# An attention kernel: a replanned order of scores, chains of five on VectorE, and first loads in halves

## The chip, the cores and the metric

The kernel runs on one core of one Trainium2 chip. The metric is the device time of one execution in microseconds; a version's time is the median of its runs. The profile's span, from the first to the last instruction, is about 1.75 us shorter than the time of the same execution (kernel before: 397.35 us of time, 395.6 of span). Each run also lists the mean clock granted to TensorE; it turns out to matter. Every run used here is in the fast state, except one single look, whose state is unknown and of which only the head is read, up to the landing of two transposes, the wait for them and the scores that follow.

## The reference

Grouped-query attention: batch 8, 8 query heads, 2 key/value heads, 1024 positions, head dimension 64, float32 in and out.

```
for g in range(n_kv_heads):
    scores = scale * np.matmul(q_group, k_group.transpose(0, 1, 3, 2))
    scores_max = np.max(scores, axis=-1, keepdims=True)
    attn = np.exp(scores - scores_max)
    attn = attn / (np.sum(attn, axis=-1, keepdims=True) + 1e-08)
    output[:, q_start:q_end, :, :] = np.matmul(attn, v_group)
```

## The kernel before

A *job* is one half of a query head (512 queries); a *cell* is one 128x512 block of its scores, 8 cells to a job, 16 to a head, 1024 in all. A cell's exponential is made by ScalarE (two cells per instruction) or by VectorE (one bit-trick instruction per cell, then a chain of four instructions over a group of cells). The score product goes into one of two double-bank buffers for ScalarE (`aps`) or one of two single banks for VectorE (`dps`). The product of the exponentials with V accumulates in `ops` and is normalised by VectorE.

Which engine takes which cell, and the order of every instruction, come from a small simulation in Python, `make_plan`, which always takes what could start first by its own table of durations. The engines then run this fixed order:

```
GROUP = 4
...
    QK, PV, EXP, P1, NORM = 0.214, 0.143, 0.925, 0.605, 0.57
    CHAIN = (0.73, 0.73, 1.26, 1.26)
    FROM_PE, FROM_ACT, FROM_DVE = 0.28, 0.18, 0.12
    LIVE_A, LIVE_D, PENDING, ONLY_A = 26, 6, 8, 14
...
            t, to_d = (ta, 0) if ta <= td else (td, 1)
            if t < INF:
                best = min(best or (INF,), (t, 1 + to_d, "qk", to_d))
```

The first head is loaded in float32 and transposed on TensorE; every later one is cast to bf16 in DRAM by a GpSimd DMA and transposed by two DMAs on the SP queue into `qT`. The head of the program, cut to what is argued about:

```
        for eng, src in ((nc.sync, k[0, 0]), (nc.scalar, q[0, 0])):
            ...                                     # one DMA each
        nc.sync.dma_start(out=vf, in_=v[0, 0]...)
        cast(("q", 0, 1), q[0, 1])                  # GpSimd queue: second head
        for two in range(2):
            nc.gpsimd.tensor_copy(out=vsets[0]..., in_=vf...)   # waits for V
        for side in range(2):
            nc.gpsimd.memset(ksets[1]..., 0.0)
        ...                                         # casts, transposes, copies of K and Q
```

The casts of the third head (0,2), of the next K and so on follow on GpSimd's queue, as planned events.

The softmax here doesn't subtract the row's maximum and nothing guards it: scores larger than these inputs give would overflow.

Of the kernel before, what the change touches and what calls it, by code (L numbers as in the profile page):

```python
# [11 lines left out]

CURVE_A, CURVE_B = 0.32988085, -0.33401025

GROUP = 4


def make_plan(nj, nkc):
# [3 lines left out]



    QK, PV, EXP, P1, NORM = 0.214, 0.143, 0.925, 0.605, 0.57
    CHAIN = (0.73, 0.73, 1.26, 1.26)
    FROM_PE, FROM_ACT, FROM_DVE = 0.28, 0.18, 0.12
    LIVE_A, LIVE_D, PENDING, ONLY_A = 26, 6, 8, 14
    INF = 1e9
    n = nj * nkc  # L30
    ops = []
    pe = act = dve = 0.0
    a_free, bank, obank_free = [0.0, 0.0], [0.0, 0.0], [0.0, 0.0]
# [12 lines left out]
    while normed < nj:  # L46
        best = None
        if nxt < n:
            ta = td = INF
            if open_a is not None:  # L50
                ta = max(pe, open_a["t"])
            elif live["A"] < LIVE_A:
                ta = max(pe, min(a_free))
            if pending < PENDING and nxt < n - ONLY_A and (cur or live["D"] < LIVE_D):
                td = max(pe, min(bank))
            t, to_d = (ta, 0) if ta <= td else (td, 1)
            if t < INF:
                best = min(best or (INF,), (t, 1 + to_d, "qk", to_d))
        for i, s in enumerate(open_jobs):
            for c in rem[s]:  # L60
                at = max(pe, ready.get(s * nkc + c, INF))
                if at < INF:
                    best = min(best or (INF,), (at, 3 + i, "pv", (s, c)))
        if len(open_jobs) < 2 and next_job < nj:
            at = max(pe, min(obank_free), min(ready.get(next_job * nkc + c, INF) for c in range(nkc)))
            if at < INF:
                best = min(best or (INF,), (at, 3 + len(open_jobs), "open", next_job))
        for q, p, kind in ((normq, 0, "norm"), (p1q, 1, "p1"), (chainq, 2, "chain")):
# [1 line left out]
                best = min(best or (INF,), (max(dve, q[0][0]), p, kind, 0))  # L70
        if cur and nxt >= n - ONLY_A and not p1q:
            best = min(best or (INF,), (dve, 9, "flush", 0))
        t, _, kind, arg = best
        if kind == "qk":
            cell = nxt
            nxt += 1
            pe = t + QK
            if not arg:
                if open_a is None:
                    slot = first_free(a_free)  # L80
                    a_id += 1
                    live["A"] += 1
                    open_a = {"slot": slot, "t": a_free[slot], "cells": []}
                    a_free[slot] = INF
                o = open_a
                ops.append((t, "qk", cell, "A", a_id, o["slot"], len(o["cells"])))
                o["cells"].append(cell)
                home[cell] = ("A", a_id)
                if len(o["cells"]) == 2 or nxt >= n:
                    act = max(act, pe + FROM_PE)  # L90
                    ops.append((act, "exp", a_id, tuple(o["cells"])))
                    act += EXP * len(o["cells"]) / 2
                    a_free[o["slot"]] = act + FROM_ACT
                    uses[("A", a_id)] = len(o["cells"])
                    for x in o["cells"]:
                        ready[x] = act + FROM_ACT
                    open_a = None
            else:
                k = first_free(bank)
                bank[k] = INF  # L100
                pending += 1
                ops.append((t, "qk", cell, "D", k, 0, 0))
                p1q.append((pe + FROM_PE, cell, k))
        elif kind == "open":
            o = first_free(obank_free)
            obank[arg] = o
            obank_free[o] = INF
            open_jobs.append(arg)
            rem[arg] = list(range(nkc))
            next_job += 1  # L110
        elif kind == "pv":
            s, c = arg
            cell = s * nkc + c
            opens = len(rem[s]) == nkc
            rem[s].remove(c)
            done = not rem[s]
            ops.append((t, "pv", s, cell, opens, done, obank[s]))
            pe = t + PV
            h = home[cell]
            uses[h] -= 1  # L120
            if not uses[h]:
                live[h[0]] -= 1
            if done:
                open_jobs.remove(s)
                normq.append((pe + FROM_PE, s))
        elif kind == "norm":
            s = normq.pop(0)[1]
            ops.append((t, "norm", s))
            dve = t + NORM
            obank_free[obank[s]] = dve + FROM_DVE  # L130
            normed += 1
        elif kind == "p1":
            _, cell, k = p1q.pop(0)
            if not cur:
                d_id += 1
                live["D"] += 1
            ops.append((t, "p1", cell, k, d_id, len(cur)))
            dve = t + P1
            bank[k] = dve + FROM_DVE
            cur.append(cell)  # L140
            home[cell] = ("D", d_id)
            if len(cur) == GROUP:
                chainq.append((dve, d_id, cur, 0))
                cur = []
        elif kind == "flush":
            chainq.append((dve, d_id, cur, 0))
            cur = []
        else:
            _, g, cells, step = chainq.pop(0)
            ops.append((t, "chain", g, len(cells), step))  # L150
            dve = t + CHAIN[step] * len(cells) / GROUP
            if step + 1 < len(CHAIN):
                chainq.insert(0, (dve, g, cells, step + 1))
            else:
                pending -= len(cells)
                uses[("D", g)] = len(cells)
                for x in cells:
                    ready[x] = dve + FROM_DVE
# [4 lines left out]
def kernel(  # L163
# [25 lines left out]
    NQS = QBS // 128  # L189
    E1 = D + 1  # L190
    PIECE = 256
    scale = 1.0 / math.sqrt(D)
    bits_scale = 128.0 * scale * math.log2(math.e)
    bits_bias = 128.0 * 127.0
# [12 lines left out]
    first_pool = ctx.enter_context(tc.tile_pool(name="firstp", bufs=1))  # L207
    qT_pool = ctx.enter_context(tc.tile_pool(name="qTpool", bufs=8))
    kT_pool = ctx.enter_context(tc.tile_pool(name="kTpool", bufs=4))
    pa_pool = ctx.enter_context(tc.tile_pool(name="papool", bufs=26))  # L210
    pd_pool = ctx.enter_context(tc.tile_pool(name="pdpool", bufs=6))
    tmp_pool = ctx.enter_context(tc.tile_pool(name="tmppool", bufs=2))
    ostage_pool = ctx.enter_context(tc.tile_pool(name="ostage", bufs=10))
    recip_pool = ctx.enter_context(tc.tile_pool(name="recip", bufs=10))
# [24 lines left out]
    qT = {}  # L239
# [48 lines left out]

    def first_loads():

        staged = []
        for eng, src in ((nc.sync, k[0, 0]), (nc.scalar, q[0, 0])):
            f = first_pool.tile([128, NHC, 2, D], FP32, name=f"f{len(staged)}")
            eng.dma_start(
                out=f, in_=src.rearrange("(c p two) d -> p c two d", p=128, two=2)
            )
            staged.append(f)
        vf = first_pool.tile([128, NHC, 2, D], FP32, name="vf")
        nc.sync.dma_start(
            out=vf, in_=v[0, 0].rearrange("(c p two) d -> p c two d", p=128, two=2)  # L300
        )
        cast(("q", 0, 1), q[0, 1])
        for two in range(2):
            nc.gpsimd.tensor_copy(
                out=vsets[0][:, 0, two * NHC : (two + 1) * NHC, 0:D],
                in_=vf[:, :, two, :],
            )
        for side in range(2):
            nc.gpsimd.memset(ksets[1][(1 - side) * D : (2 - side) * D, :, side, :], 0.0)  # L309
        fk, fq = staged  # L310

        hk = first_pool.tile([128, NHC, 3, D], BF16, name="hk")
        nc.vector.tensor_copy(out=hk[:, :, 0:2, :], in_=fk)  # L313
        nc.vector.tensor_copy(out=hk[:, :, 2, :], in_=fk[:, :, 0, :])
        hq = first_pool.tile([128, NHC, 2 * D], BF16, name="hq")
        nc.scalar.copy(out=hq, in_=fq.rearrange("p c two d -> p c (two d)"))
        tk = dbanks[0].tile([128, 2, HALF], BF16, name="dps0")
        tq = dbanks[1].tile([128, HALF], BF16, name="dps1")
        for w in range(2):
            for c in range(NHC):  # L320
                nc.tensor.transpose(  # L321
                    tk[:, w, c * 128 : (c + 1) * 128],
                    hk[:, c, w : w + 2, :].rearrange("p w d -> p (w d)"),
                    ident,
                )
        for c in range(NHC):
            nc.tensor.transpose(tq[:, c * 128 : (c + 1) * 128], hq[:, c, :], ident)
        qT[(0, 0)] = qT_pool.tile([128, HALF], BF16, name="qT")
        lo, hi = slice(0, D), slice(D, 2 * D)
        nc.vector.tensor_copy(out=ksets[0][lo, 0, 0, 0:HALF], in_=tk[lo, 0, :])  # L330
        nc.scalar.copy(out=qT[(0, 0)], in_=tq)
        nc.vector.tensor_copy(out=ksets[0][lo, 0, 0, HALF:S], in_=tk[lo, 1, :])
        nc.vector.tensor_copy(out=ksets[0][hi, 0, 1, 0:HALF], in_=tk[hi, 1, :])
        nc.vector.tensor_copy(out=ksets[0][hi, 0, 1, HALF:S], in_=tk[hi, 0, :])

    p_of = {}
    psum = {}
# [168 lines left out]
```

## Time and profile before

| | before |
|---|---|
| time, median of 4 runs | 397.99 us (397.90 to 398.06) |
| span of the profiled run | 395.6 us |
| ScalarE busy, idle before its exponentials | 381.5 us, 2.1 us |
| VectorE busy, TensorE busy | 375.8 us, 365.7 us |
| first exponential starts, last one ends | 8.16 us, 388.22 us |

In a line of a group, the columns are: source line, engine, operation, output and input tiles with their shapes, count, then busy time in us and mean duration in ns, then idle time of the engine just before these instructions and what ended most of it. The prediction shows these lines.

### The profile page before, as it was taken

Reading aid. Unit: us, or ns where it says so; the run is one execution under the profiler, and the core shown is the slowest. Engines: PE = TensorE matmul, PEld = TensorE weight load, DVE = VectorE, ACT = ScalarE, POOL = GpSimd, SP = SyncE. Lnnn points to the kernel's source line nnn. Section 1 sums busy time; section 2 is a strip of 40 time slices with the busy share of each in tenths; the row PEclk is TensorE's granted clock in tenths of the full one; section 3 lists DMA queues with packets and bytes.
Section 4 is the critical chain, followed back from the end, with each engine's and each line's share of the span. In section 5 each row is a group of like instructions: output and inputs, shape, how many; then the busy total and the mean of one; then the engine's idle time right before and its main releaser. Section 6 shows DMA issues by size and latency. Waiting matters only on the chain.

```text
span 395.6 us, 12683 instructions
## 1 busy us (share of the span) xinstructions
PE 365.7 (92%) x5043; PEld 233.0 (59%) x5132; DVE 375.8 (95%) x664; ACT 381.5 (96%) x415; POOL 86.6 (22%) x165
## 2 busy tenths in 40 slices
PE   4899999999999999999999999999999999999986
PEld 2455566565656556655656565565655666565655
DVE  4999999999999999999999999999999999999995
ACT  4999999999999999999999999999999999999992
POOL 5340303132041313113131040312214131120000
PEclk9999999999999999999999999999999999999999
DMA  4665866749676786847758686785965867574314
GB/s 106 106 125 111 163 107 127 128 86 160 103 139 130 132 143 101 142 90 145 115 103 141 111 141 112 118 143 98 155 109 115 149 132 121 99 130 99 68 28 94
DMA packets 134890, 46.72 MB, mean 118 GB/s; under 512 B 130848, under 2 KB 132384, under 8 KB 133344
## 3 DMA queue, kind: packets, MB, share of 16 engines
q1 hardware_dynamic: 129408, 29.52, 38.3%
q0 software_dynamic: 4896, 16.13, 27.0%
q8 instruction: 40, 0.66, 0.8%
q10 hardware_dynamic: 528, 0.26, 0.2%
q14 instruction: 18, 0.15, 0.2%
HBM read 27.13 MB, written 28.97 MB: 142 GB/s over the span
## 4 chain that ended last, share of the span: by engine, by line
ACT 67%; DVE 11%; PE 10%; issue 6%; DMA 3%; POOL 1%; SPq 0%
ACT pa L362 67%; PE ops L414 5%; PE aps L351 5%; DVE pd L371 3%; DVE y L402 2%; DVE pd L406 2%; DVE ost L429 1%; DMA vf<-in_v_dram 1%; PE dps L351 1%; DVE y L392 1%; DMA qT<-scr_q 1%; POOL kset L309 1%; DVE z L386 1%; DVE rec L427 1%; DMA scr_q<-in_q_dram 1%
## 5 line engine op out<-in xcount | busy, mean ns | idle before, releaser
L362 ACT ACTIVATE pa<-aps 128x1024 bf16<-128x1024 f32 x412 | 379.0, 1064 | 2.1 <-PE aps L351 1.3
L351 PE MATMUL aps<-qT,kset 128*128 128x512 bf16 x735 | 226.2, 379 | 15.5 <-ACT pa L362 13.6
L414 PEld LDWEIGHTS <-pa 128*128 128x128 bf16 x3296 | 134.5, 97 | 57.6 <-DVE ost L429 0.8
L414 PE MATMUL ops<-vset,pa 128*128 128x65 bf16 x3296 | 143.9, 193 | 3.4
L371 DVE TENSOR_SCALAR pd<-dps 128x512 uint16<-128x512 f32 x200 | 129.8, 682 | 2.2 <-PE dps L351 2.2
L351 PEld LDWEIGHTS <-kset 128*128 128x128 bf16 x1024 | 85.3, 97 | 66.3 <-issue 30.9
L248 POOL DMA_DIRECT2D scr_q<-in_q_dram x63 | 34.0, 540 | 173.4 <-PE aps L351 150.6
L351 PE MATMUL dps<-qT,kset 128*128 128x512 bf16 x200 | 64.5, 380 | 1.0
L406 DVE TENSOR_TENSOR pd<-pd,y 128x2048 uint16<-128x2048 uint16 x50 | 61.2, 1225 | 1.7
L402 DVE TENSOR_TENSOR y<-z,y 128x2048 f16<-128x2048 uint16 x50 | 61.2, 1225 | 1.7
L429 DVE TENSOR_TENSOR ost<-ops,rec 128x256 f32<-128x256 f32 x128 | 54.3, 425 | 4.4
L414 PEld LDWEIGHTS <-pd 128*128 128x128 bf16 x800 | 38.5, 97 | 29.8 <-DVE pd L406 7.9
L268 POOL DMA_DIRECT2D kset<-kT x60 | 32.2, 545 | 76.7 <-DMA kT<-scr_k 68.7
L414 PE MATMUL ops<-vset,pd 128*128 128x65 bf16 x800 | 45.3, 194 | 1.2
L392 DVE TENSOR_SCALAR y<-z 128x2048 f16<-128x2048 uint16 x50 | 34.3, 687 | 0.6
L386 DVE TENSOR_SCALAR z<-pd 128x2048 uint16<-128x2048 uint16 x50 | 34.2, 684 | 0.0
L427 DVE RECIPROCAL rec<-ops 128x4 f32<-128x4 f32 x128 | 22.6, 176 | 2.4 <-PE ops L414 1.9
L248 POOL DMA_DIRECT2D scr_v<-in_v_dram x15 | 7.6, 505 | 8.2 <-PE aps L351 7.1
L248 POOL DMA_DIRECT2D scr_k<-in_k_dram x15 | 8.1, 542 | 4.7 <-PE aps L351 4.3
L321 PE MATMUL dps<-ident,hk 128*128 128x128 bf16 x8 | 1.0, 311 | 5.0 <-DVE hk L313 5.0
L321 PEld LDWEIGHTS <-hk 128*128 128x128 bf16 x8 | 0.8, 141 | 5.0 <-DVE hk L313 5.0
L309 POOL MEMSET kset<- 64x2048 bf16 x2 | 3.6, 1798 | 0.1
(20 smaller groups left out, 9.7 us busy)
## 6 DMA issues: line engine op xcount, KB each, us to landing
out_dram<-ost SPq DMA_DIRECT2D x128, 128.0 KB, 3.2
scr_q<-in_q_dram POOLq DMA_DIRECT2D x63, 128.0 KB, 3.5
kset<-kT POOLq DMA_DIRECT2D x60, 64.0 KB, 2.7
qT<-scr_q SPq DMA_TRANSPOSE x126, 3.6
scr_k<-in_k_dram POOLq DMA_DIRECT2D x15, 128.0 KB, 4.2
scr_v<-in_v_dram POOLq DMA_DIRECT2D x15, 128.0 KB, 3.9
vset<-scr_v SPq DMA_DIRECT2D x30, 64.0 KB, 3.8
kT<-scr_k SPq DMA_TRANSPOSE x30, 3.4
```

The costliest lines, as they stand in the source:

```text
L248: dma = nc.gpsimd.dma_start(out=scr.rearrange("(p f) -> p f", f=1024), in_=src.rearrange("(p s) d -> p (s d)", s=1024 // D),)
L268: nc.gpsimd.dma_start(out=ksets[b % 2][side * D : (side + 1) * D, g, side, parity * HALF : (parity + 1) * HALF], in_=kT[(b, g)][parity * D ...
L351: last_score[0] = nc.tensor.matmul(dst, lhsT=ksets[b % 2][:, h // HPG, side, c * 128 : (c + 1) * 128], rhs=qT[(b, h)], start=True, stop=Tr ...
L362: nc.scalar.activation(out=pt[:, 0:m], in_=psum.pop(("A", n))[:, 0:m], func=AF.Exp, scale=scale)
L371: nc.vector.tensor_scalar(out=groups[g][:, slot], in0=psum.pop(cell), scalar1=bits_scale, scalar2=bits_bias, op0=ALU.mult, op1=ALU.add,)
L386: nc.vector.tensor_scalar(out=z, in0=pd, scalar1=0x7F, scalar2=None, op0=ALU.bitwise_and)
L392: nc.vector.tensor_scalar(out=y, in0=temps[g][0], scalar1=CURVE_A / 128.0, scalar2=CURVE_B, op0=ALU.mult, op1=ALU.add,)
L402: nc.vector.tensor_tensor(out=y, in0=z, in1=y, op=ALU.mult)
L406: nc.vector.tensor_tensor(out=pd, in0=pd, in1=y, op=ALU.add)
L414: nc.tensor.matmul(ops_of[s][:, qs, :], lhsT=p_of[cell][:, qs * 128 : (qs + 1) * 128], rhs=vsets[b % 2][:, h // HPG, c, :], start=opens an ...
L427: nc.vector.reciprocal(out=rec, in_=o[:, :, D])
L429: nc.vector.tensor_tensor(out=ost, in0=o[:, :, 0:D], in1=rec.unsqueeze(2).to_broadcast([128, NQS, D]), op=ALU.mult,)
```

## The change

Its intent: plan with durations that match the machine, so that planned gaps of ScalarE go away; let a score for ScalarE be preferred although its bank is free up to 0.08 us later; spread the fixed cost of VectorE's chains over five cells; give VectorE fewer cells near the end; start the first exponential sooner by loading the first K and Q in halves, with 28 idle products meant to bring TensorE to full pace before the first scores. Cut to its core:

```diff
-GROUP = 4
+GROUP = 5
-    QK, PV, EXP, P1, NORM = 0.214, 0.143, 0.925, 0.605, 0.57
-    CHAIN = (0.73, 0.73, 1.26, 1.26)
+    QK, PV, P1, NORM = 0.216, 0.122, 0.605, 0.57
+    EXP, CHAIN = (0.067, 0.4267), ((0.20, 0.133),) * 2 + ((0.19, 0.27),) * 2
-    LIVE_A, LIVE_D, PENDING, ONLY_A = 26, 6, 8, 14
+    LIVE_A, LIVE_D, PENDING, ONLY_A, AHEAD, FIRST_PV = 32, 5, 7, 26, 0.08, 2.0
-                best = min(best or (INF,), (t, 1 + to_d, "qk", to_d))
+                early = 0.0 if to_d else AHEAD
+                best = min(best or (INF,), (t - early, 1 + to_d, "qk", to_d, t))
 ... (buffers for 32 and 5 live tiles; EXP and CHAIN as fixed cost plus cost per cell)
-            eng.dma_start(out=f, in_=src...)
+            for half in halves:
+                eng.dma_start(out=f[:, half], in_=src...[:, half])
-        cast(("q", 0, 1), q[0, 1])
         for two in range(2):
             nc.gpsimd.tensor_copy(out=vsets[0]..., in_=vf...)
+        cast(("q", 0, 1), q[0, 1])
         for side in range(2):
             nc.gpsimd.memset(ksets[1]..., 0.0)
+        for n in range(WARM):                       # WARM = 28
+            nc.tensor.matmul(warm, lhsT=ident, rhs=ident, start=True, stop=True)
 ... (casts, transposes and copies of K and Q by halves)
```

More of the change, by code (lines that the diff above doesn't have):

```diff
@@ L57, in make_plan @@
             if t < INF:
-                best = min(best or (INF,), (t, 1 + to_d, "qk", to_d))
+                early = 0.0 if to_d else AHEAD
+                best = min(best or (INF,), (t - early, 1 + to_d, "qk", to_d, t))
         for i, s in enumerate(open_jobs):
             for c in rem[s]:
-                at = max(pe, ready.get(s * nkc + c, INF))
+                at = max(pe, FIRST_PV, ready.get(s * nkc + c, INF))
                 if at < INF:
@@ L64, in make_plan @@
         if len(open_jobs) < 2 and next_job < nj:
-            at = max(pe, min(obank_free), min(ready.get(next_job * nkc + c, INF) for c in range(nkc)))
+            at = max(pe, FIRST_PV, min(obank_free), min(ready.get(next_job * nkc + c, INF) for c in range(nkc)))
             if at < INF:
@@ L72, in make_plan @@
             best = min(best or (INF,), (dve, 9, "flush", 0))
-        t, _, kind, arg = best
+        t, _, kind, arg = best[:4]
         if kind == "qk":
+            t = best[4]
             cell = nxt
@@ L91, in make_plan @@
                     ops.append((act, "exp", a_id, tuple(o["cells"])))
-                    act += EXP * len(o["cells"]) / 2
+                    act += EXP[0] + EXP[1] * len(o["cells"])
                     a_free[o["slot"]] = act + FROM_ACT
@@ L150, in make_plan @@
             ops.append((t, "chain", g, len(cells), step))
-            dve = t + CHAIN[step] * len(cells) / GROUP
+            dve = t + CHAIN[step][0] + CHAIN[step][1] * len(cells)
             if step + 1 < len(CHAIN):
@@ L191 @@
     PIECE = 256
+    WARM = 28
     scale = 1.0 / math.sqrt(D)
@@ L209 @@
     kT_pool = ctx.enter_context(tc.tile_pool(name="kTpool", bufs=4))
-    pa_pool = ctx.enter_context(tc.tile_pool(name="papool", bufs=26))
-    pd_pool = ctx.enter_context(tc.tile_pool(name="pdpool", bufs=6))
+    pa_pool = ctx.enter_context(tc.tile_pool(name="papool", bufs=32))
+    pd_pool = ctx.enter_context(tc.tile_pool(name="pdpool", bufs=5))
     tmp_pool = ctx.enter_context(tc.tile_pool(name="tmppool", bufs=2))
@@ L289, in first_loads @@
     def first_loads():
-        staged = []
-        for eng, src in ((nc.sync, k[0, 0]), (nc.scalar, q[0, 0])):
-            f = first_pool.tile([128, NHC, 2, D], FP32, name=f"f{len(staged)}")
-            eng.dma_start(
-                out=f, in_=src.rearrange("(c p two) d -> p c two d", p=128, two=2)
-            )
-            staged.append(f)
-        vf = first_pool.tile([128, NHC, 2, D], FP32, name="vf")
-        nc.sync.dma_start(
-            out=vf, in_=v[0, 0].rearrange("(c p two) d -> p c two d", p=128, two=2)
-        )
-        cast(("q", 0, 1), q[0, 1])
+        fk = first_pool.tile([128, NHC, 2, D], FP32, name="fk")
+        fq = first_pool.tile([128, NHC, 2, D], FP32, name="fq")
+        vf = first_pool.tile([128, NHC, 2, D], FP32, name="vf")
+        rows = "(c p two) d -> p c two d"
+        halves = (slice(0, NHC // 2), slice(NHC // 2, NHC))
+        for eng, f, src in ((nc.sync, fk, k[0, 0]), (nc.scalar, fq, q[0, 0])):
+            for half in halves:
+                eng.dma_start(
+                    out=f[:, half], in_=src.rearrange(rows, p=128, two=2)[:, half]
+                )
+        nc.sync.dma_start(out=vf, in_=v[0, 0].rearrange(rows, p=128, two=2))
         for two in range(2):
@@ L307, in first_loads, with turn_k @@
             )
+        cast(("q", 0, 1), q[0, 1])
         for side in range(2):
             nc.gpsimd.memset(ksets[1][(1 - side) * D : (2 - side) * D, :, side, :], 0.0)
-        fk, fq = staged
+        warm = obanks[1].tile([128, 128], FP32, name="ops1")
+        for n in range(WARM):
+            nc.tensor.matmul(warm, lhsT=ident, rhs=ident, start=True, stop=True)
         hk = first_pool.tile([128, NHC, 3, D], BF16, name="hk")
-        nc.vector.tensor_copy(out=hk[:, :, 0:2, :], in_=fk)
-        nc.vector.tensor_copy(out=hk[:, :, 2, :], in_=fk[:, :, 0, :])
         hq = first_pool.tile([128, NHC, 2 * D], BF16, name="hq")
-        nc.scalar.copy(out=hq, in_=fq.rearrange("p c two d -> p c (two d)"))
         tk = dbanks[0].tile([128, 2, HALF], BF16, name="dps0")
         tq = dbanks[1].tile([128, HALF], BF16, name="dps1")
-        for w in range(2):
-            for c in range(NHC):
+        qT[(0, 0)] = qT_pool.tile([128, HALF], BF16, name="qT")
+        lo, hi = slice(0, D), slice(D, 2 * D)
+        def turn_k(w, half):
+            for c in range(NHC)[half]:
                 nc.tensor.transpose(
@@ L325, in first_loads, with put_k @@
                 )
-        for c in range(NHC):
-            nc.tensor.transpose(tq[:, c * 128 : (c + 1) * 128], hq[:, c, :], ident)
-        qT[(0, 0)] = qT_pool.tile([128, HALF], BF16, name="qT")
-        lo, hi = slice(0, D), slice(D, 2 * D)
-        nc.vector.tensor_copy(out=ksets[0][lo, 0, 0, 0:HALF], in_=tk[lo, 0, :])
-        nc.scalar.copy(out=qT[(0, 0)], in_=tq)
-        nc.vector.tensor_copy(out=ksets[0][lo, 0, 0, HALF:S], in_=tk[lo, 1, :])
-        nc.vector.tensor_copy(out=ksets[0][hi, 0, 1, 0:HALF], in_=tk[hi, 1, :])
-        nc.vector.tensor_copy(out=ksets[0][hi, 0, 1, HALF:S], in_=tk[hi, 0, :])
+        def put_k(side, parity, half):
+            part = (lo, hi)[side]
+            cols = slice(half.start * 128, half.stop * 128)
+            nc.vector.tensor_copy(
+                out=ksets[0][part, 0, side, parity * HALF : (parity + 1) * HALF][:, cols],
+                in_=tk[part, side ^ parity, cols],
+            )
+        for half in halves:
+            nc.vector.tensor_copy(out=hk[:, half, 0:2, :], in_=fk[:, half])
+            turn_k(0, half)
+            nc.scalar.copy(
+                out=hq[:, half], in_=fq[:, half].rearrange("p c two d -> p c (two d)")
+            )
+            for c in range(NHC)[half]:
+                nc.tensor.transpose(tq[:, c * 128 : (c + 1) * 128], hq[:, c, :], ident)
+        nc.scalar.copy(out=qT[(0, 0)], in_=tq)
+        nc.vector.tensor_copy(out=hk[:, :, 2, :], in_=fk[:, :, 0, :])
+        put_k(0, 0, slice(0, NHC))
+        turn_k(1, slice(0, NHC))
+        put_k(0, 1, slice(0, NHC))
+        put_k(1, 0, slice(0, NHC))
+        put_k(1, 1, slice(0, NHC))
     p_of = {}
```

## The prediction

> **What bounds the kernel now.** I read the busy table first, then the groups of instructions, then the waits, then the timeline at both ends. The work is 1024 score tiles of 128x512 ("cells"). 824 of them get their exponential from ScalarE, two per instruction; 200 from VectorE, by one bit-trick instruction each and a chain of four instructions per group of four.
>
> ```profile
> PE 365.7 (92%) x5043; PEld 233.0 (59%) x5132; DVE 375.8 (95%) x664; ACT 381.5 (96%) x415; POOL 86.6 (22%) x165
> ...
> L362 ACT ACTIVATE pa<-aps 128x1024 bf16<-128x1024 f32 x412 | 379.0, 1064 | 2.1 <-PE aps L351 1.3
> ...
> L371 DVE TENSOR_SCALAR pd<-dps 128x512 uint16<-128x512 f32 x200 | 129.8, 682 | 2.2 <-PE dps L351 2.2
> ...
> L406 DVE TENSOR_TENSOR pd<-pd,y 128x2048 uint16<-128x2048 uint16 x50 | 61.2, 1225 | 1.7
> ...
> L392 DVE TENSOR_SCALAR y<-z 128x2048 f16<-128x2048 uint16 x50 | 34.3, 687 | 0.6
> ```
>
> All three compute engines look full, so the share does not decide. The idle column does: the 412 exponentials of ScalarE have only 2.1 us of idle before them in the whole run. The waits view says the same from the other side:
>
> ```profile
> PE aps L351 <- ACT pa L362: 13.6, 44, 0.6
> ...
> ACT pa L362 <- PE aps L351: 1.3, 2, 1.1
> ```
>
> TensorE waits 13.6 us for ScalarE to free a score buffer, ScalarE waits 1.3 us for TensorE. So between its first and last exponential the kernel is a ScalarE stream. Its step: the last 15 exponentials take 13.91 us (below), so one step is (13.91 - 1.06) / 14 = 0.918 us; the duration of 1064 ns overlaps its neighbour. Over the run from 19.02 us, where 401 exponentials are left, the mean step is (388.22 - 1.06 - 19.02) / 400 = 0.920 us. That middle holds about 400 x 0.002 = 1 us to win, no more.
>
> ```profile
> 1.32 0.62 POOL L248 DMA_DIRECT2D scr_q<-in_q_dram  x1 [0.20 <-issue]
> ...
> 4.93 0.62 ACT L316 CAST hq<-f 128x512 bf16<-128x512 f32 x1 [2.40 <-DMA f<-in_q_dram]
> ...
> 5.96 0.74 POOL L304 CAST vset<-vf 128x256 bf16<-128x256 f32 x2 [3.62 <-DMA vf<-in_v_dram]
> ...
> 6.17 9.48 SPq L260 DMA_TRANSPOSE qT<-scr_q  x4
> ...
> 6.48 0.58 ACT L331 COPY qT<-dps 128x512 bf16<-128x512 bf16 x1 [0.93 <-PE dps L327]
> ...
> 7.11 1.86 PE L351 MATMUL aps<-qT,kset 128*128 128x512 bf16 x4 [0.67 <-ACT qT L331]
> ...
> 8.16 10.67 ACT L362 ACTIVATE pa<-aps 128x1024 bf16<-128x1024 f32 x11 [1.10 <-PE aps L351]
> ```
>
> ```profile
> 374.31 13.91 ACT L362 ACTIVATE pa<-aps 128x1024 bf16<-128x1024 f32 x15
> ...
> 389.18 2.63 PE L414 MATMUL ops<-vset,pa 128*128 128x65 bf16 x80
> ...
> 392.06 0.42 DVE L429 TENSOR_TENSOR ost<-ops,rec 128x256 f32<-128x256 f32 x1
> ```
>
> Three stages follow: a head of 8.16 us before the first exponential, the stream, and a tail of 395.6 - 388.22 = 7.4 us, in which TensorE works off output products that had piled up (4.3 us to the end of the last normalisation at 392.48, then 3.1 us of store).
>
> [...] The trace has 918 ns; its figure is used. [...] the first four score products step (1.86 - 0.63) / 3 = 0.41 us, later pairs show 0.21. [...] this trace's cast of a Q head issued at 10.37 us landed at 13.25, so 2.9 us. [...]
>
> **The change, part by part.**
>
> *Shares.* Running both planners gives, before, 824 cells on ScalarE and 200 on VectorE; after, 828 and 196. ScalarE gets 414 exponentials: 2 x 0.918 = +1.84 us on the bound.
>
> *Chains of five.* VectorE: 196 x 0.649 (129.8 / 200) = 127.2; 39 chains of 2 x (0.686 + 0.133) + 2 x (1.225 + 0.267) = 4.62 each, 180.2; one chain of a single cell, about 1.4 by the same slopes; normalisation unchanged, 76.9 (54.3 + 22.6). Sum 385.7, against 129.8 + 191 + 76.9 = 397.7. So 12 us leave VectorE. But it was not the bound, and the plan does not turn the time into more VectorE cells; it gives it fewer. Worth 0 directly.
>
> *Waiting a moment for a score bank, better constants.* These take planned bubbles out: the planner's mean distance of two exponentials goes from 0.949 to 0.926 us. But the machine already ran at 0.920, below the old plan, since in-order queues run ahead of planned bubbles. I take 0.9195 after, half the possible win: 400 x 0.0008 = -0.3 us.
>
> *Tail.* The old plan ends its last normalisation 6.03 us after the last exponential starts (the machine: 392.48 - 387.16 = 5.3). The new plan has 2.74: 16 cells of output products remain, at 4 x (2.63 - 0.19) / 79 = 0.123 us each, 2.0 us, then 0.28 and 0.6 of normalisation. The store adds 3.1. So last start to end is 5.85 instead of 8.4: -2.6 us.
>
> *Head, the first exponential.* The cast of Q head (0,1) no longer competes with the first loads, so I put the second half of Q at 4.5 us (before, the whole landed at 4.93). Cast of half the width 0.40 [...], 0.26 to reach TensorE as before, two transposes instead of four 0.42, copy 0.04 + 0.58, 0.05: first score at 6.25. With the 28 idle products having warmed the clock, two scores take 0.6: first exponential at 6.9 us, -1.26. It cannot be shorter by much, as the loads themselves are the wait.
>
> *Head, the second Q head.* The order of the changed kernel's instructions has, on GpSimd: copies of V, then the cast of Q head (0,1), then two memsets. Before, this cast was issued at 1.32, ahead of everything. The copies wait for V; V landed at 5.96 and I put it at 5.5 now. Copies 0.74, so the cast is issued at 6.3 and lands at 9.2 (2.9 as above). The two DMA transposes follow at 9.2 and 10.4 (1.2 each on the queue) and the second lands 2.4 later, at 12.8. Cell 16 is the first that needs it. The new plan has it 4.70 us after the first score, so at 6.25 + 4.70 = 10.95. Only five exponentials can run before: 6.9 + 5 x 0.92 = 11.5. ScalarE then sits idle until 12.8 plus 0.21 and 0.63 for three scores: the sixth exponential starts at 13.65 instead of 11.5. This new wait of 2.1 us eats the head's gain and more.
>
> **Sum.** Sixth exponential 13.65; 408 further steps of 0.9195 = 375.2, so the last starts at 388.85; plus 5.85 = 394.7 us of span. Before, the median time is 398.0 - 395.6 = 2.4 above the span. 394.7 + 2.4 = 397.1; I say 397.0.
>
> **Rivals.**
> 1. *No new wait at the second head*, because V lands much earlier or the transposes are quick. Then the sixth exponential starts at 11.5, and the time is 2.1 less, 395.0. For it: the removed cast frees the DMA engines. Against: V would have to land at about 3.4 us, earlier than K did before (4.49).
> 2. *The new order starves ScalarE.* TensorE's queue is in order: a VectorE score placed too early waits for its bank and holds up the scores of ScalarE behind it. Chains of five hold VectorE for 4.6 us instead of 3.8, with two banks. If each of 39 chains cost 0.2 us, 8 us come on top: 405. For it: eight or so steps of before already show about 0.25 us of such a loss. Against: the plan's distances for VectorE agree with the trace (0.605 per bit-trick; 1.28 for a pair on the timeline), and VectorE gets 12 us more room.
> 3. *VectorE had been the true bound* and the shorter chains pay in full, 12 us, 386. The idle columns speak against it: ScalarE would have to show waits, and has 2.1 us. And 414 steps of 0.918 = 380 plus a head of 6.9 and a tail of at least 4.8 give 391.7 of span, 394 of time: a floor under any version with this split.
>
> **Range.** The known terms (-1.3 head, -2.6 tail, +1.8 exponentials, -0.3 steps, +2.1 new wait) give -0.3; with the old head's own small losses before the sixth exponential gone (about 0.6), -0.9, which is the sum above. The wait at the second head can be 1 us less or 1.5 more, steps 1 us either way: 394.5 to 399.5. Faster by over 2% needs under 390, below the floor: 0.01. Slower by over 2% needs rival 2 in full: 0.02.
>
> **What would show it.** In the profile after: ScalarE's group x414 with about 0.92 us a step; in the waits, ScalarE or the score products waiting 1 to 3 us for the transfer of qT, once, near 11 to 13 us; first exponential near 6.9; VectorE busy near 365 us with chains of 0.82 and 1.49 us; the last normalisation under 3 us after the last exponential starts. It is wrong if ScalarE shows no wait for qT before 14 us, if its step rises above 0.93, or if the tail stays at 7 us.

## The result, and the profile after

The changed kernel takes 400.50 us (median of 4 runs, 399.33 to 401.40) against 397.99: ratio 1.0062, 95% interval 1.0035 to 1.0088. It is slower, by 0.6%, clear of noise and within 2%. The prediction said 397.0, and 394.5 to 399.5: the measured median lies above the range. Ratios here are the mean time of one kernel's fast runs over that of the other's in the same rounds, so not quite the ratio of the quoted medians.

The busy table and the groups of the page after:

```profile
PE 374.0 (94%) x5160; PEld 234.2 (59%) x5160; DVE 368.8 (92%) x621; ACT 384.3 (96%) x418; POOL 89.6 (22%) x165
...
L383 ACT ACTIVATE pa<-aps 128x1024 bf16<-128x1024 f32 x414 | 381.6, 1062 | 7.2 <-PE aps L372 6.1
```

VectorE is 7 us less busy and has gained nothing for the kernel. ScalarE has 414 exponentials, as the plan said, and its idle time before them is 7.2 us instead of 2.1. So the place to look is where ScalarE waits. The view of waits (waiting engine, tile and line, releaser, us in total, times, longest):

```profile
ACT pa L383 <- PE aps L372: 6.1, 5, 4.3
...
PE dps L372 <- DMA qT<-scr_q: 3.4, 1, 3.4
```

One wait of 4.3 us on ScalarE, behind one wait of 3.4 us of TensorE for a transposed Q. The timeline of the head (start us, us, engine, line, operation, tiles, count, idle before and releaser):

```profile
4.63 0.40 ACT L344 CAST hq<-fq 128x256 bf16<-128x256 f32 x1 [0.41 <-DMA fq<-in_q_dram]
...
5.79 0.75 POOL L306 CAST vset<-vf 128x256 bf16<-128x256 f32 x2 [4.43 <-DMA vf<-in_v_dram]
...
6.15 1.53 PE L372 MATMUL aps<-qT,kset 128*128 128x512 bf16 x4
...
6.48 0.64 POOL L251 DMA_DIRECT2D scr_q<-in_q_dram  x1
...
7.20 2.85 ACT L383 ACTIVATE pa<-aps 128x1024 bf16<-128x1024 f32 x3 [1.10 <-PE aps L372]
...
9.46 6.64 SPq L263 DMA_TRANSPOSE qT<-scr_q  x4
...
15.00 0.59 PE L372 MATMUL dps<-qT,kset 128*128 128x512 bf16 x1 [3.45 <-DMA qT<-scr_q]
...
16.48 1.02 ACT L383 ACTIVATE pa<-aps 128x1024 bf16<-128x1024 f32 x1 [4.30 <-PE aps L372]
...
17.77 1.02 ACT L383 ACTIVATE pa<-aps 128x1024 bf16<-128x1024 f32 x1 [0.27 <-PE aps L372]
...
19.06 5.92 ACT L383 ACTIVATE pa<-aps 128x1024 bf16<-128x1024 f32 x6 [0.27 <-PE aps L372]
```

The first exponential is 0.96 us earlier than before (7.20 against 8.16). But GpSimd issues the second head's cast only at 6.48, behind the copies of V that wait for V until 5.79; before, it was issued at 1.32. The transposes start at 9.46 instead of 6.17, and the first cell of the second head runs at 15.00. ScalarE sits idle for 4.3 us. TensorE kept to the order of its queue meanwhile: output products of exponentials that had ended by 12.18 us (10.24 + 1.94) started only at 16.23, behind the scores that waited. Then ScalarE's sixth and seventh exponentials are 1.29 us apart instead of 0.92. The sums over the stretch from 10 to 21 us say why. Columns: stretch and length, then for PE, PEld, DVE, ACT and POOL the busy us and the count, then granted TensorE clock, DMA share, GB/s; first the kernel before, then the changed one:

```profile
10.00:21.00 11.00, 9.62 (x100) 5.13 (x101) 10.53 (x18) 10.65 (x13) 3.48 (x7) 1.00 0.61 103
```

```profile
10.00:21.00 11.00, 7.29 (x49) 3.46 (x48) 7.06 (x8) 5.98 (x7) 4.14 (x7) 0.69 0.99 102
```

ScalarE loses 4.7 us of work (10.65 - 5.98). TensorE's mean clock is 0.69; it is 0.52 from 14 to 15 us and 0.50 from 15 to 20: the clock fell back to half during the wait, and the products after it ran slow (two scores from 15.38 took 1.06 us, two from 10.37, before the wait, 0.59). And the DMA engines are busy for 0.99 of this stretch, against 0.61, for the same bytes per second.

The other end did what was expected:

```profile
379.15 15.76 ACT L383 ACTIVATE pa<-aps 128x1024 bf16<-128x1024 f32 x17
...
396.22 0.42 DVE L450 TENSOR_TENSOR ost<-ops,rec 128x256 f32<-128x256 f32 x1
```

The last exponential starts at 379.15 + 15.76 - 1.06 = 393.85 and the last normalisation ends at 396.64, 2.79 us later; before, it was 5.3. The span ends at 399.6.

### The profile page after: what moved, and what is told of

It is laid out like the page before. It is cut to its first block, busy times and chain, and to the rows that moved or that the text cites. A ratio compares the mean times of both kernels' runs of the same rounds, so it can differ in the third digit from the quotient of the medians.

```text
span 399.6 us, 12764 instructions
## 1 busy us (share of the span) xinstructions
PE 374.0 (94%) x5160; PEld 234.2 (59%) x5160; DVE 368.8 (92%) x621; ACT 384.3 (96%) x418; POOL 89.6 (22%) x165
## 4 chain that ended last, share of the span: by engine, by line
ACT 73%; PE 17%; issue 5%; DMA 3%; SPq 1%; POOL 0%; DVE 0%
ACT pa L383 73%; PE aps L372 9%; PE ops L435 6%; PE dps L372 2%; DMA qT<-scr_q 1%; DMA vf<-in_v_dram 1%; DMA scr_q<-in_q_dram 1%; SPq L263 0%; SPq L301 0%; POOL vset L306 0%; DVE ost L450 0%; DVE rec L448 0%
## 5 line engine op out<-in xcount | busy, mean ns | idle before, releaser
L372 PE MATMUL aps<-qT,kset 128*128 128x512 bf16 x828 | 248.1, 381 | 16.9 <-ACT pa L383 14.1
L435 PEld LDWEIGHTS <-pa 128*128 128x128 bf16 x3312 | 137.4, 98 | 56.3 <-DVE ost L450 2.2
L435 PE MATMUL ops<-vset,pa 128*128 128x65 bf16 x3312 | 149.6, 194 | 0.0
L372 PE MATMUL dps<-qT,kset 128*128 128x512 bf16 x196 | 67.6, 379 | 3.4 <-DMA qT<-scr_q 3.4
L423 DVE TENSOR_TENSOR y<-z,y 128x2560 f16<-128x2560 uint16 (+1 forms) x40 | 58.5, 1464 | 1.1
L427 DVE TENSOR_TENSOR pd<-pd,y 128x2560 uint16<-128x2560 uint16 (+1 forms) x40 | 58.5, 1463 | 1.0
L435 PE MATMUL ops<-vset,pd 128*128 128x65 bf16 x784 | 49.3, 193 | 0.0
L407 DVE TENSOR_SCALAR z<-pd 128x2560 uint16<-128x2560 uint16 (+1 forms) x40 | 32.4, 810 | 0.7
L413 DVE TENSOR_SCALAR y<-z 128x2560 f16<-128x2560 uint16 (+1 forms) x40 | 32.3, 806 | 0.2
L316 PE MATMUL ops<-ident 128*128 128x128 bf16 x28 | 3.2, 313 | 1.4 <-POOL ident masks.py:199 1.4
```

The source lines that it names most:

```text
L372: last_score[0] = nc.tensor.matmul(dst, lhsT=ksets[b % 2][:, h // HPG, side, c * 128 : (c + 1) * 128], rhs=qT[(b, h)], start=True, stop=Tr ...
L407: nc.vector.tensor_scalar(out=z, in0=pd, scalar1=0x7F, scalar2=None, op0=ALU.bitwise_and)
L413: nc.vector.tensor_scalar(out=y, in0=temps[g][0], scalar1=CURVE_A / 128.0, scalar2=CURVE_B, op0=ALU.mult, op1=ALU.add,)
L423: nc.vector.tensor_tensor(out=y, in0=z, in1=y, op=ALU.mult)
L427: nc.vector.tensor_tensor(out=pd, in0=pd, in1=y, op=ALU.add)
L435: nc.tensor.matmul(ops_of[s][:, qs, :], lhsT=p_of[cell][:, qs * 128 : (qs + 1) * 128], rhs=vsets[b % 2][:, h // HPG, c, :], start=opens an ...
```

## The experiments

"The second head" is Q head (0,1), "the third" is (0,2). Medians are given with the kernel before of the same call. All results were correct.

| run | us (runs) | before | ratio, 95% interval |
|---|---|---|---|
| e1_early_cast | 398.56 (6) | 397.64 | 1.0029, 1.0012 to 1.0046 |
| e2_old_head | 397.84 (6) | 397.64 | 1.0004, 0.9991 to 1.0017 |
| e3_old_plan | 400.54 (6) | 397.64 | 1.0073, 1.0050 to 1.0095 |
| e4_old_plan_early | 399.74 (6) | 397.64 | 1.0053, 1.0029 to 1.0076 |
| f1_hold_casts | 406.49 (1) | 397.56 | one look |
| f2_late_zero | 396.97 (5) | 397.56 | 0.9986, 0.9973 to 0.9999 |
| f3_no_warm | 397.17 (5) | 397.56 | 0.9991, 0.9977 to 1.0004 |
| f4_no_ahead | 401.67 (4) | 397.56 | 1.0104, 1.0090 to 1.0117 |
| g1_before_late_zero | 401.89 (6) | 397.62 | 1.0103, 1.0087 to 1.0119 |
| g2_group4 | 402.56 (4) | 397.62 | 1.0113, 1.0098 to 1.0128 |
| g3_group8 | 398.18 (5) | 397.62 | 1.0012, 1.0000 to 1.0024 |
| h1_before_third | 397.28 (5) | 397.66 | 0.9996, 0.9984 to 1.0009 |
| h2_third | 397.17 (5) | 397.66 | 0.9987, 0.9974 to 0.9999 |
| h3_third_group4 | 399.22 (5) | 397.66 | 1.0037, 1.0024 to 1.0049 |
| h4_third_old_plan | 396.51 (5) | 397.66 | 0.9971, 0.9957 to 0.9984 |

### Head or plan? Four kernels

**e1**, the changed kernel with one line moved back:

```diff
+        cast(("q", 0, 1), q[0, 1])
         for two in range(2):
             nc.gpsimd.tensor_copy(...)
-        cast(("q", 0, 1), q[0, 1])
```

> The changed kernel with one line moved: the cast of Q head (0,1) is issued ahead of the copies of V again, as in the kernel before. Theory (the late cast makes TensorE and ScalarE wait for that head, 4.3 us, and the wait lets TensorE's clock fall back): no wait for qT before the sixth exponential, which starts near 12.1 us instead of 16.48, no stretch at half clock after the head; the third head, whose cast still stands behind the GpSimd memsets, then holds the twelfth exponential to about 18.9 us, so not all is won: 396.0 to 397.5 us against 400.5. Rival (the new plan's order costs the time in the stream): 399.5 to 400.5.

**e2**, the new plan with the first loads of before (`first_loads` swapped whole, no warm-up):

> The new plan with the first loads of the kernel before. Theory (head alone costs): 397.0 to 398.3 us, as the shorter tail of 2.6 us pays for two more exponentials (1.8) and a step that is 0.002 us longer (0.8): no worse than before. Rival (the plan costs): 399.5 or more.

**e3**, the kernel before with the new first loads, cast late:

> The old plan with the new first loads, cast late. Theory: the wait of 3 to 4 us for the second head stands here too, with the old tail: 400.5 to 402 us, and a TensorE clock below 1.0 in some runs. Rival (the plan costs, the head gains): 396.5 to 397.5.

**e4**, the same as e3 with the cast early:

> The old plan with the new first loads, but the cast early. Theory: the second head comes in time, the third holds the twelfth exponential to about 18.9 us, where the kernel before had 19.02, so the earlier first exponential (near 7.2 instead of 8.16) is lost again: 397.3 to 398.2 us. If the earlier start were worth its 1 us to the end: 397.0 or less.

The head alone makes the loss: with the old plan it costs 0.73% (e3), and its clock is below 1.0 in four of six runs (0.991 to 0.996), as the theory said. The new plan alone costs nothing that can be told (e2, 1.0004). So the rival is out as the cause of this loss.

But moving one cast back recovers only part: e1 was expected at 396.0 to 397.5 and took 398.56; e4 was expected at 397.3 to 398.2 and took 399.74. The timeline of ScalarE in e1 shows the rest:

```profile
7.50 2.89 ACT L383 ACTIVATE pa<-aps 128x1024 bf16<-128x1024 f32 x3 [0.68 <-PE aps L372]
10.90 7.60 ACT L383 ACTIVATE pa<-aps 128x1024 bf16<-128x1024 f32 x8 [0.52 <-PE aps L372]
19.97 4.91 ACT L383 ACTIVATE pa<-aps 128x1024 bf16<-128x1024 f32 x5 [1.47 <-PE aps L372]
```

The wait for the second head is gone, and the twelfth exponential, the first with a cell of the third head, waits until 19.97, later even than in the kernel before (19.02). The third head's cast stands behind two GpSimd memsets of 3.65 us and is issued at 10.82. I had expected this wait, but to end at 18.9. In e4 the same wait (TensorE idle for 1.63 us) was followed in the profiled run by a stretch at about half clock (0.57 from 19 to 23 us), and ScalarE's next two steps are 1.74 and 1.65 us:

```profile
19.59 1.02 ACT L381 ACTIVATE pa<-aps 128x1024 bf16<-128x1024 f32 x1 [1.55 <-PE aps L370]
21.33 1.02 ACT L381 ACTIVATE pa<-aps 128x1024 bf16<-128x1024 f32 x1 [0.71 <-PE aps L370]
22.98 1.95 ACT L381 ACTIVATE pa<-aps 128x1024 bf16<-128x1024 f32 x2 [0.63 <-PE aps L370]
```

Five of its six runs have the mean clock of this one, 0.996. In e1, where TensorE was idle for 1.5 us, one run of six has it (400.34 us). That I had not expected.

### Why the second head came later than worked out

**f1** asks only for the landing of the second head. All other casts are held:

```diff
-  at(th - 28.0, cast, ("q", b, h), ...)
+  at(max(th - 28.0, 6.0), cast, ("q", b, h), ...)
 ... (the casts of K and V and the later transposes likewise)
```

> The changed kernel, but all casts except that of Q head (0,1) are held until the scores of the second head run (so the kernel is slower on purpose at the third head; only the landing of the second head's transposes is asked). Theory (the second transpose took 4.2 us to land instead of 2.4 because the burst of casts on the GpSimd queue shares the DMA engines): it lands 2.3 to 2.6 us after its issue, and cell 16 starts near 13.1 us instead of 15.0. Rival (the transposes are slow there for another reason): 4 us again and cell 16 near 15.

The view of the tile qT between 8.5 and 12 us holds just these two transposes; the last line is the time from issue to landing (minimum, median, maximum). First the changed kernel, then f1:

```profile
DMA to landing us min/median/max: 2.3/3.2/4.2
```

```profile
DMA to landing us min/median/max: 2.3/2.4/2.5
```

Issued at the same times, the second one lands in 2.5 us instead of 4.2 when no burst of casts runs beside it, and the first cell of the second head starts at 13.27 instead of 15.00. So the burst is what delayed it. (The 406 us are from the third head's casts held on purpose.)

### The rest of the head, and parts of the plan

**f2**: e1, and the memsets moved into the stream at plan time 20.

> As the run with the early cast, and the two GpSimd memsets of the other K set (3.65 us) moved from the head to plan time 20, so that the cast of the third head is issued near 7.2 us instead of 10.8. Theory (after the second head, the third is the next wait): the twelfth exponential starts near 17.9 us instead of 19.97, no wait for qT, and 396.0 to 397.0 us against 398.56; the first version at or below the kernel before. Rival (the stream of the new plan gives it back): 398 or more.

**f3**: f2 with `WARM = 0`.

> The same without the 28 idle products. If they are worth something: [...] the third and fourth exponentials come late as with the old head (steps of 1.6 to 1.7 us there), 0.7 to 2.0 us more than the run with them. If ScalarE's pace hides the slow clock: within 0.4 us.

**f4**: f2 with `AHEAD = 0.0`.

> The same as the late memsets, with the plan's head start for ScalarE's scores set to 0 (the part 'a score may wait a moment for its bank' undone): 199 cells on VectorE, 413 exponentials, a planned tail of 1.9 instead of 2.7 us, but planned steps of 0.942 instead of 0.926. If the machine closes planned bubbles as it did in the kernel before: 1 to 1.7 us less. If the bubbles are real: steps rise by 0.005 or more, 1 us or more longer.

In f2 there is no wait for qT; from its fourth exponential at 10.64 on, fifteen follow at 0.933 us (14.12 us in all), so the twelfth starts near 18.1. At 396.97 it is 0.14% faster than the kernel before: the first version whose interval lies below 1, if narrowly. The 28 idle products show 0.2 us (f3), within the intervals; without them ScalarE idles 1.10 us before its first exponential instead of 0.68, and its fourth starts at 10.70 instead of 10.64.

f4 was a surprise in its size. The lines of ScalarE at both ends:

```profile
11.18 13.27 ACT L381 ACTIVATE pa<-aps 128x1024 bf16<-128x1024 f32 x14 [0.52 <-PE dps L370]
...
379.27 16.43 ACT L381 ACTIVATE pa<-aps 128x1024 bf16<-128x1024 f32 x18
```

Without the head start ScalarE has one exponential less, but its step from the 4th (11.18) to the 396th (379.27) is 368.09 / 392 = 0.939 (0.923 in f2), where this plan had foreseen 0.942: the planned gaps were real, and 4.7 us were lost. The same planner with the old constants had planned 0.949 and the machine ran 0.920.

### A control that failed, and what it showed

**g1**: the kernel before with only the memsets moved to plan time 20. **g2**: f2 with `GROUP = 4`. **g3**: f2 with chains of eight and other limits (eight pending, the last 32 cells on ScalarE, head start 0.06).

> The kernel before with only the two GpSimd memsets moved from the head to plan time 20: the control for the best version so far (396.97). If that version's gain came from the memsets alone: 396.7 to 397.1 us here. If the head in halves and the new plan carry it: the twelfth exponential gains only its wait of 0.3 us, 397.2 to 397.6, no clear difference to the kernel before.

> The best version so far with chains of four cells instead of five, all else as it is. Its plan has 193 cells on VectorE, 416 exponentials, steps of 0.9275, and ends 3.2 us later. If planned bubbles are real with these constants: 399.5 to 400.5 us. If the machine runs ahead of them: 397.0 to 398.5 (two more exponentials and half a microsecond of tail).

> The best version so far with chains of eight, eight cells pending, the last 32 cells on ScalarE and a head start of 0.06: 198 cells on VectorE, 413 exponentials, a plan that ends 0.55 us earlier. If the plan's end tells the machine's: 396.2 to 396.8 us. If longer chains hold the two VectorE banks too long: above 397.5.

g1 should have been near 397 by either theory and took 401.89. The timeline of VectorE in g1, while the two memsets run on GpSimd (28.55, 4.08 us), and the same chain in the kernel before:

```profile
29.29 1.60 DVE L384 TENSOR_SCALAR z<-pd 128x2048 uint16<-128x2048 uint16 x1
30.93 2.25 DVE L390 TENSOR_SCALAR y<-z 128x2048 f16<-128x2048 uint16 x1
```

```profile
28.70 0.68 DVE L386 TENSOR_SCALAR z<-pd 128x2048 uint16<-128x2048 uint16 x1
29.42 0.69 DVE L392 TENSOR_SCALAR y<-z 128x2048 f16<-128x2048 uint16 x1
```

The same two instructions took 2.5 us longer beside a memset: 1.60 and 2.25 us against 0.68 and 0.69. What in the machine makes them wait is not shown. TensorE then waited 2.5 us for the chain, and ScalarE for TensorE. The clock fell here too: after the wait two scores of g1 took 1.04 us, before it 0.59, and the mean clock is below 1.0 in five of six runs of g1 (0.994 to 0.996) and in three of four of g2 (0.994 and 0.995). The one run of g1 at 1.0 took 400.03 us. So g1, g2 and g3 tell nothing of what they were built for (g2 and g3 show the same wait of TensorE for the chain between 30 and 40 us, 1.7 and 1.4 us); f2 only lost 0.75 us on one instruction, 1.57 us beside a memset against 0.82. They are told here because a "free" place for work on an idle engine turned out not to be free.

### The head mended without memsets in the stream

All four have the third head's cast ahead of the memsets, which stay in the head:

```diff
         for two in range(2):
             nc.gpsimd.tensor_copy(...)
+        cast(("q", 0, 2), q[0, 2])
         for side in range(2):
             nc.gpsimd.memset(ksets[1]...)
 ... (and the planned cast of this head is left out)
```

**h1** is the kernel before with this edit. **h2** is the changed kernel with this edit and that of e1. **h3** is h2 with `GROUP = 4`. **h4** is e4 with this edit: new first loads, both casts early, old plan.

> The kernel before with the cast of Q head (0,2) issued ahead of the two GpSimd memsets, which stay in the head: a clean control in place of the one whose memsets fell among VectorE's chain. Only the twelfth exponential's wait of 0.3 us is to be had: 397.2 to 397.6 us, no clear difference to the kernel before. If the third head's cast alone carries the best version's gain: 396.9 or less.

> The changed kernel with two casts moved: that of head (0,1) ahead of the copies of V, that of head (0,2) ahead of the memsets. Theory (the order of GpSimd's queue in the head, and nothing else, made the change lose): no wait for qT, twelfth exponential near 18.0 us, TensorE's clock 1.0 in every run, 396.0 to 397.0 us. Rival (something else in the new head or plan costs as well): 397.6 or more.

> The same with chains of four. Its plan ends 3.2 us later than that of five. If planned bubbles are real with the new constants: 2.5 to 3.5 us above the run with five. If the chain length is free: within 1 us of it.

> The new first loads with both casts early, and the old plan: the head in halves alone. Theory: the first exponential near 7.3 us instead of 8.16 and no later wait, so 0.5 to 1.0 us under the kernel before: 396.6 to 397.1. Against the run with the new plan it then shows what the plan is worth: theory within 0.5 us of it.

h2 takes 397.17 us; the changed kernel, in another call, took 400.50 (ratios to the kernel before: 0.9987 and 1.0062): two casts placed earlier are worth 0.75%, 3 us, and turn a loss into a small gain. Its clock is 1.0 in all five runs. The expectation had 396.0 to 397.0, a little low. h1 shows that the edit alone does nothing measurable to the kernel before.

h4 is the best, 396.51 us, 0.29% under the kernel before, and that is the old plan. The timeline of ScalarE at its start:

```profile
8.19 16.72 ACT L382 ACTIVATE pa<-aps 128x1024 bf16<-128x1024 f32 x18 [1.15 <-PE aps L371]
```

Eighteen exponentials without a wait, one every (16.72 - 1.06) / 17 = 0.921 us. The first is no earlier than before (8.19 against 8.16) in this profiled run; the gain is that nothing after it waits long enough to show, neither for the clock nor for the third head. So its twelfth starts near 18.3, against 19.02 in the kernel before. In h1, the old head, the third and fourth exponentials wait for TensorE:

```profile
8.29 1.94 ACT L363 ACTIVATE pa<-aps 128x1024 bf16<-128x1024 f32 x2 [1.10 <-PE aps L352]
10.85 1.02 ACT L363 ACTIVATE pa<-aps 128x1024 bf16<-128x1024 f32 x1 [0.62 <-PE aps L352]
12.25 12.13 ACT L363 ACTIVATE pa<-aps 128x1024 bf16<-128x1024 f32 x13 [0.38 <-PE aps L352]
```

Of the two causes expected, an earlier first exponential and no later wait, only the second came, so it is partly luck that the gain came near the expected size (0.5 to 1.0 us). One thing that held the first exponential back was overlooked: on GpSimd the early cast stands ahead of the last step of the identity matrix that the idle products read. So they start at 2.4 us instead of 1.41, and VectorE's copies of K then wait 2.1 us in sum for their transposes, in the changed kernel 1.1. h4 without the idle products was not run.

Chains of four instead of five cost 2.05 us (h3 against h2), between the two things expected. The step is not longer: 368.06 / 399 = 0.922 from the 4th exponential (11.23) to the 403rd (379.29). Two more exponentials (416 for 414) account for 2 x 0.918 = 1.84 us. So, as far as these two runs show, the chain of five pays because it leaves VectorE room for three more cells, not because it closes gaps.

## Why the prediction was wrong, point by point

**Right: the bound.** ScalarE's stream with its count of exponentials and steps near 0.92 us sets the time. VectorE's 7 us less (12 were predicted; its busy time fell from 375.8 to 368.8) are worth nothing by themselves. The chain itself came as worked out: 0.823 + 0.820 + 1.490 + 1.489 = 4.62 us for five cells, against 0.684 + 0.687 + 2 x 1.225 = 3.82 for four, so the fifth cell adds 0.14 and 0.13 us to the instructions on one tensor and 0.26 to those on two (0.133 and 0.267 were put in); the chain of a single cell took 0.28 + 0.28 + 0.43 + 0.42 = 1.41.

**Right: the tail.** Predicted 5.85 us from the last start to the end, measured 399.6 - 393.85 = 5.75.

**Right in kind, off by 0.3: the first exponential.** The second half of Q was there at 4.63 (predicted 4.5), its cast took 0.40 us as put, and V was there at 5.79 (5.5; in e1, with the cast of the second head early, 6.41). The first score came at 6.15 (predicted 6.25), but the four first scores took 1.53 us, (1.53 - 0.38) / 3 = 0.38 us from one to the next, so mostly at the half pace of the start still (0.41 in the kernel before), although TensorE had been at work since 1.41; the exponential began at 7.20 instead of 6.9. The granted clock is listed as 1.00 at the start of both kernels: it is the pace of the scores that shows this. "With the 28 idle products having warmed the clock" was wrong in this run. In e1, e4, f1, f2 and h2 it held: there ScalarE idles 0.68 us before its first exponential instead of 1.10, and in f2 the four scores took 1.02 us, (1.02 - 0.38) / 3 = 0.21 from one to the next.

**The step that failed: "the second lands 2.4 later, at 12.8".** The mechanism was right: the new wait is where the prediction put it, behind the copies of V. Its size was not. V's copies, the cast and the first transpose all came within 0.3 us of the working. The second transpose took 4.2 us to land, not 2.4. I had taken 2.4 from the kernel before, where these two transposes ran with the queues empty (a DMA share of 0.00 from 6 to 7 us, as the first is issued). The late cast moves them into the burst of casts for later heads, which the trace of before shows from 10.37 us on, and which I did not put beside them. f1 shows it: without the burst 2.5 us, and the cell starts at 13.27. The sixth exponential came at 16.48 instead of 13.65: 2.83 us, where the range had allowed 1.5.

**A consequence that was left out: the clock.** TensorE idle for 3.45 us fell back to half rate (a granted clock of 0.50 from 15 to 20 us), and the two steps after the wait took 2.58 us instead of 1.84. The spread of the runs follows from it: the changed kernel took 399.33 us in its run at a clock of 1.0, 400.35 and 400.64 at 0.996, 401.40 at 0.991. The kernel before stays within 0.16 us in the same rounds. As an estimate from these runs, the clock accounts for 400.50 - 399.33 = 1.2 us of the 3.5 us between the predicted and the measured median; only the run at 401.40 was profiled. The length of one wait does not tell whether the clock falls: in e4 it fell after TensorE had been idle for 1.63 us in one piece (busy 1.11 us in the 3 us from 16 to 19) and in g2 with a wait of 1.7; after f1's wait of 1.91 us two scores took 0.59, full pace, and the profiled run of e1 has a mean clock of 1.0 with a wait of 1.5. What decides it is not shown.

**The second step that failed: "I take 0.9195 after".** From the 8th exponential (19.06) to the last (393.85), 406 steps took 0.923 us each, 1.5 us more than predicted in sum, and above the 0.920 of before. The reason that I gave, in-order queues running ahead of planned gaps, failed for the new plan. My explanation, argued and not shown, is that it holds only for a plan with padded durations. The old plan counted 0.143 us for an output product that takes 0.123, so its gaps need not appear on the machine. The new constants are nearer to the machine, and the plan's gaps, 0.9256 - 0.9204 = 0.005 us per step, are of the size that the machine shows above 0.918. f4 supports this with larger gaps (planned 0.942, measured 0.939). Chains of four (h3) do not fit it: planned 0.9275, measured 0.922, so a plan with longer gaps ran with shorter steps. What makes up the last 0.003 us of the step stays open.

**A smaller error the other way.** The time is 1.75 us above the span of the same run, not 2.4; I had subtracted the profiled run's span from the median of others.

Sum for the profiled run: 16.48 + 377.4 + 5.75 + 1.8 = 401.4 us, against 13.65 + 375.2 + 5.85 + 2.4 = 397.1.

**What the parts are worth, from the runs.** The late cast and the memsets ahead of the third: 0.75% (changed kernel against h2). The new plan with a mended head: 0.66 us slower than the old plan (h2 against h4, whose intervals just overlap), with the old head no difference (e2); its shorter tail (-2.6 us) is eaten by two more exponentials and a longer step. The head in halves with both casts early and the old plan: 1.15 us, 0.29% (h4).

## What to carry to other kernels

When a change moves an issue behind something that waits, follow the transfer to its last user, and time it among the traffic of its new place, not with the duration it had in its old one. Look also at what one stall does next: here a wait of 3.5 us cost TensorE its clock as well, 0.50 for the next 5 us. And do not count on the machine closing a plan's gaps because it did so under an older plan: with constants nearer to the machine, f4 lost most of what its plan foresaw.
